# Low halves and the norm's scale and bias in a two-stage trunk: from GpSimd to VectorE

## The chip, the core and the metric

The kernel runs on one NeuronCore of a Trainium2 chip. The metric is the device time of one execution in microseconds (us); the time of a kernel is the median of its timed runs. TensorE (PE) multiplies, VectorE (DVE), ScalarE (ACT) and GpSimd (POOL) work elementwise, SyncE (SP) issues most transfers. Each engine takes its instructions in order; semaphores order the engines among themselves.

## What is computed

A post-norm decoder layer on 512 tokens of 1024 channels: a mixer of three branches, an output projection, a residual and a layer norm; then a two-level mixture of 16 experts, a residual and a second norm. Everything is float32. Cut to what matters here:

```python
def reference(x, mem, ...):
    x = layer_norm(x, ln_in_g, ln_in_b)
    m = hybrid_mixer(x, ...)                      # ends in y @ w_o + b_o
    x = layer_norm(ALPHA * x + m, ln1_g, ln1_b)   # "the norm" of the change
    f = hierarchical_moe(x, w_rg, b_rg, w_re, b_re, w_up, w_down)
    x = layer_norm(ALPHA * x + f, ln2_g, ln2_b)

def hierarchical_moe(x, ...):
    # best of 4 groups, best 2 of its 4 experts, weights from the two softmaxes
    h = silu(x @ w_up[e][:, :256]) * (x @ w_up[e][:, 256:]) * gate[e]
    y = sum over e of h @ w_down[e]
```

## The kernel before

**Split products.** Each float32 matrix is split into a high half (a cast to fp32r, on ScalarE) and a low half (the matrix less its high half). A product is three TensorE passes: high times high, high times low, low times high (`mm3`). For an expert's up weights, four slices of 128x1024, `prep_hi` casts and `prep_lo` subtracts (L691); for its down weights, two slices, `dn_hi` casts and `dn_lo` subtracts (L1142). The tokens of a block are split in `split_xs`, the hidden activations in `h_ev` (both through L82 on ScalarE and L83 on VectorE).

**Output projection and norm.** The loop over `i` from 0 to 7 makes eight tiles of 128 tokens x 512 channels; tile i is half n = i // 4 of token tile i % 4. `wo_mm` issues its 24 multiplications in pieces, `wo_add` (L719) adds the residual on VectorE, `wo_stats` (L725) takes the statistics. One iteration later TensorE transposes the tile (`r_tr`, which therefore waits for `wo_add`) and multiplies it into the router's logits (`router`). From i = 5 on the second half of a token tile t is there, and VectorE makes its inverse deviation (`ln1_stats`), the logits (`logits_a`, `logits_b`), the centering times gain (`center_ops`, L822) and the scale plus bias (`scale_ops`, L826). In the kernel before, only token tile 0 takes that way whole: tile 1 is centered on VectorE, scaled on ScalarE (L873) and biased on GpSimd (L874); tile 2 and three quarters of tile 3 go through `ln1_act`, normed on ScalarE (L837), multiplied by the gain and biased on GpSimd (L838, L839). `put_x1` stores a normed tile twice in device memory: for the gathers, and as the residual of the second norm. `prep_half(0, ...)` prepares expert 0's four slices in iterations 5 and 6, its low halves on GpSimd.

**Routing.** `route_ops` finds the group and the two experts of each token in short chains on VectorE; `rank_mm` counts on TensorE; `pos_ops` makes the positions of the last expert's tokens, the first block's; `pick` multiplies these tokens out of x1 (L812) instead of gathering them. `weave(chain, fill)` issues a chain of small operations with large ones spread between them.

**Experts.** 18 blocks of 128 places follow: experts in `order`, two of them twice. Block b multiplies up (`up_mm`, 24 multiplications L109), transposes the hidden activations of the block before (`h_tr`, L1116), transposes the tokens of the next (`transp`, L1095), and multiplies the block before down (`down_mm`, L1153). In between VectorE and ScalarE prepare the next expert's slices, gate the hidden activations (L1110), and order the remaining experts and tokens by load (`order_experts`, `order_tokens`; L1045 to L1070, L1216 to L1237). GpSimd gathers the tokens of a later block by indices (L1018) and scatters a finished block into the sum in device memory (L1166). In the kernel before it also makes the low halves of slices 0 and 3 of expert 1, of slices 2 and 3 of expert 2, and of the down weights of experts 0 and 1.

**Order.** From L697 on the order is written out by hand (`manual_schedule`): each engine runs what the program lists, in that order. Loads of weights are 1 MB units on SyncE's queue (`load_unit`, L674); a load that reuses a buffer waits for its last reader.

Of the kernel before, what the change touches and what calls it, by code (L numbers as in the profile page):

```python
# [17 lines left out]
P = 128  # L18
D = 1024
# [34 lines left out]
def trunk(ctx, tc, x, mem, rows, cols, wz, wkv, pac, pb8, pb2, wax, ws, wo, wr, br, we, out):  # L54
# [88 lines left out]
    def weave(chain, fill=()):  # L143
        done = 0
        for i, f in enumerate(chain):
            f()
            while done * len(chain) < (i + 1) * len(fill):
                fill[done]()
                done += 1
# [543 lines left out]
    def prep_half(key, i, lo_eng=None):  # L693
        prep_hi(key, i)
        prep_lo(key, i, lo_eng)
# [25 lines left out]
    def wo_stats(i):  # L721
        n, t = divmod(i, NT)
        if n == 0:
            stats[t] = small.tile([P, 2, 6], F32, name="bnst1", bufs=4)
        dve.bn_stats(stats[t][:, n, :], x1[:, t, n * 512:(n + 1) * 512])  # L725
# [95 lines left out]
    def center_ops(t, n, cs):  # L821
        return [lambda c=c: dve.scalar_tensor_tensor(x1[:, t, c:c + n], x1[:, t, c:c + n], mvs[t][:, 0:1], g1[:, c:c + n],  # L822
                                                     op0=ALU.subtract, op1=ALU.mult) for c in cs]
# [5 lines left out]
    def put_x1(eng, t):  # L829
        for d_ in (x1_d, acc_d[0]):  # L830
            eng.dma_start(d_[t * P:(t + 1) * P, :], x1[:, t, :])

    def ln1_act(t, c0):
        nmr = small.tile([P, 1], F32, name="nmr", bufs=2)
        dve.scalar_tensor_tensor(nmr, mvs[t][:, 0:1], -1.0, rstds[t], op0=ALU.mult, op1=ALU.mult)
        hb = x1[:, t, c0:]
        act.activation(hb, hb, AF.Identity, scale=rstds[t], bias=nmr)  # L837
        pool.tensor_tensor(hb, hb, g1[:, c0:], op=ALU.mult)  # L838
        pool.tensor_tensor(hb, hb, b1[:, c0:], op=ALU.add)  # L839

    rest = []
    pending = {NT: [(2, 1)], NT + 1: [(3, 0), (3, 1)], NT + 2: [(4, 0)]}
    for i in range(2 * NT):
        j = i - 1
        t = j - NT
        ps = mmps()
        if i == 6:
            ohe = so2.tile([P, NT, P], F32, name="xr2")
        wo_mm(i, ps, 0, 2)
        if i:  # L850
            r_tr(j)
        if i in (NT + 1, NT + 2):
            for h in range(2):
                prep_half(0, 2 * (i - NT - 1) + h, pool)
        wo_mm(i, ps, 2, 4)
        if i:
            router(j)
        if t == 0:
            weave(ln1_stats(0))
        elif t == 1:  # L860
            weave(ln1_stats(1), scale_ops(0, 256, range(0, D, 256)))
            put_x1(sp, 0)
        elif t == 2:
            ops, r_ = route_ops(0, 2)
            rest += r_
            weave(ops, ln1_stats(2))
        if t >= 0:
            logits_a(t)
            if t < 2:
                weave(center_ops(t, D, (0,)))  # L870
            logits_b(t)
            if t == 1:
                act.mul(x1[:, t, :], x1[:, t, :], rstds[t])  # L873
                pool.tensor_tensor(x1[:, t, :], x1[:, t, :], b1, op=ALU.add)  # L874
                put_x1(sp, t)
            if t == 2:
                ln1_act(t, 0)
                put_x1(sp, t)
        wo_mm(i, ps, 4, 6)
        if t == 2:  # L880
            rank_mm(0)
            rank_mm(1)
            ops, r_ = route_ops(2, 3)
            rest += r_
            weave(ops, pos_ops(0, 2)[:2])
        wo_mm(i, ps, 6, 8)
        for e, u in pending.get(i, ()):
            load_unit(e, u)
        wo_add(i, ps)
        wo_stats(i)  # L890
        if i + 3 < 2 * NT:
            load_xr(i + 3)
    t = NT - 1
# [7 lines left out]
    pick(1, 4, 8)  # L901
    logits_a(t)
    logits_b(t)
    ln1_act(t, 256)
    ops, rest = route_ops(t, NT)
    weave(ops, center_ops(t, 256, (0,)) + scale_ops(t, 256, (0,)))
    put_x1(sp, t)
    pick(2, 0, 4)
    rank_mm(t)
# [47 lines left out]
    xsm = {}  # L957
    xg_ = yp.tile([P, NT, D], F32, name="y")
    xgs = [mo.tile([P, D], F32, name="xg0")] + [xg_[:, i, :] for i in range(2)]
    prep_lo(1, 0, pool)  # L960

    def scratch(shape):
        t = rt.tile([P, 128], F32, name="scr", bufs=2)
# [68 lines left out]
    def order_experts():  # L1032
# [48 lines left out]
        lambda: dve.tensor_copy(whi, wt),  # L1081
        lambda: dve.tensor_copy(val[:, 1], whi.bitcast(F32)),
        lambda: dve.tensor_tensor(val[:, 2], wt, whi.bitcast(F32), op=ALU.subtract),
    ] + vals_s + oe_a, [lambda i=i, c=c: prep_lo(1, i, None, c, c + 512) for i in (1, 2) for c in (0, 512)])
    prep_lo(1, 3, pool)
    load_unit(4, 1)

    def transp(key):
# [153 lines left out]
    for b in range(nb):  # L1242
        p_ = seq[b]
        nxt = seq[b + 1] if b + 1 < nb else p_
        pu = up_mm(b)
        if b == 0:
            dn_hi(0, 0)
            dn_hi(0, 1)
            transp(1)
            pw = map_mm(ohs_s, NS, 1, 3)  # L1250
            gws = map_gw(pw, NS, "s")
        elif b == 1:
            pth = h_tr(h)
        else:
            hT = h_ev(pth)
        if b == 3:
            blk["ixx"] = map_ix(pix, NCOLX, "x")
            gather(5, *where(5)[::2])
            gather(6, *where(6)[::2])
            weave(vals_x)  # L1260
            pwx = map_mm(ohs_x, NCOLX, 1, 3)
        if b == 4:
            blk["gwx"] = map_gw(pwx, NCOLX, "x")
        ix, gw, c = where(b)
        new = [seq[b - 1]] if b and (b == 1 or seq[b - 2] != seq[b - 1]) else []
        if b == nb - 1:
            break

        def dn_prep():
            for p1 in new:  # L1270
                pl = pools[p_] if nxt != p_ else xp if pools[p_] is hlp else hlp
                for n in range(2):
                    if b > 1:
                        dn_hi(p1, n)
                    dn_lo(p1, n, pool if b < 3 else dve, pl)
                if at[p1] + 3 < E:
                    load_unit(order[at[p1] + 3], 2)

        dn_prep()
        tail = []  # L1280
        if b == 1:
            load_unit(order[5], 0)
        if b and nxt != p_:
            for i in range(3):
                prep_hi(nxt, i)
        if 3 < b < nb - 1:
            yb = down_ev(pdn[b - 2])
        held = b > 1 and seq[b - 2] == seq[b - 1]
        if b and nxt != p_:
            if not held:  # L1290
                prep_hi(nxt, 3)
            if b == 1:
                prep_lo(nxt, 2, pool)
                prep_lo(nxt, 3, pool)
                ops = oe_b + order_tokens()
                weave(ops[:8], [lambda i=i, c=c_: prep_lo(nxt, i, None, c, c + 512) for i in range(2) for c_ in (0, 512)])
                hT = h_ev(pth)
                weave(ops[8:18])
                tail = ops[18:]
            else:  # L1300
                ops = []
                if b == 2:
                    ohs_x, ops, vals_x = map_ops(blk["px"], blk["ohx"], NCOLX, "x")
                weave(ops[:5] or [lambda: None] * 3, [lambda i=i: prep_lo(nxt, i) for i in range(3)])
                tail = ops[5:] if held else ops[5:] + [lambda: prep_lo(nxt, 3)]
        if b and nxt != p_:
            for i in (2 * at[p_] + 9, 2 * at[p_] + 10):
                if i < 2 * E:
                    load_unit(order[i // 2], i % 2)
        h = gate_h(pu, gw, c)  # L1310
        if 0 < b < nb - 1:
            transp(b + 1)
        weave(tail)
        if b + 4 < nb and b not in (1, 2):
            gather(b + 4, *where(b + 4)[::2])
        if b == nb - 2:
            gb2 = mlate.tile([P, 2048], F32, name="raw3")
            g2, b2 = gb2[:, :D], gb2[:, D:]

            def load_gb(eng, i):  # L1320
                r = ROWS.index("ln2_g") + i
                eng.dma_start((g2, b2)[i], rows[r:r + 1, :].to_broadcast([P, D]))

            load_gb(sp, 0)
            load_gb(sp, 1)
        if 3 < b < nb - 1:
            scatter(yb, *where(b - 2)[::2], b - 2)
        if b == nb - 4:
            oht = mox.tile([P, 4, T], F32R, name="rawx", bufs=2)
            row_hot(oht[:, 0], *where(nb - 3)[::2])  # L1330
        if b == nb - 3:
            for i in range(1, 3):
                row_hot(oht[:, i], *where(nb - 3 + i)[::2])
        if b:
            pdn[b - 1] = down_mm(b - 1, hT)
            if b == nb - 2:
                ys.append(down_split(pdn[b - 1]))
            elif b < 3:
                scatter(down_ev(pdn[b - 1]), *where(b - 1)[::2], b - 1)
        if b:  # L1340
            pth = h_tr(h)
        if held:
            prep_half(nxt, 3)
        if b == 2:
            pix = map_mm(ohs_x, NCOLX, 0, 1)
# [191 lines left out]
```

## Time and profile before

| | us |
|---|---|
| median of 3 timed runs (lowest, highest) | 967.24 (965.01, 968.96) |
| span of the profiled execution | 964.1 |
| TensorE busy with multiplications | 886.1 |
| VectorE busy | 617.2 |
| ScalarE busy | 456.8 |
| GpSimd busy | 155.6 |

The profile gives no time of the profiled execution apart from its span; the timed runs stand for it. Shares of busy time are averages over stages with different limits, so the stretch of the change (683 to 781 us) is read by itself. A busy engine may also be waiting inside an instruction: an instruction's length has to be held against others of its shape. The granted clock of TensorE is a share of 2.4 GHz; its two levels are 1.2 and 2.4 GHz. A wait is put down to the releaser that came last.

### The profile page before, as it was taken

The numbers are of one execution on the slowest core, as the hardware profiler recorded it, in microseconds if no ns is written. First come the engines' busy times: TensorE is split into PE (matmuls) and PEld (weight loads), VectorE is DVE, ScalarE is ACT, GpSimd is POOL, SyncE is SP. The second block draws the span as 40 slices with busy tenths as digits, with TensorE's granted clock in tenths as the row PEclk, the third lists the DMA queues.
The fourth block names the chain that finished last, engine by engine and source line by source line (L and its number), as shares of the span: only waits on it lengthen the run. The fifth ranks groups of instructions, "written<-read, shape, count | busy, mean of one in ns | idle before, by whom it ended". The sixth has DMA issues, their size and how long they took to land. (4 is left out here: it accounts for less than half of the span.)

```text
span 964.1 us, 11210 instructions
## 1 busy us (share of the span) xinstructions
PE 886.1 (92%) x4260; PEld 739.1 (77%) x4260; DVE 617.2 (64%) x993; ACT 456.8 (47%) x635; POOL 155.6 (16%) x112
## 2 busy tenths in 40 slices
PE   4798999999999999999999999999965789999990
PEld 3586888889988888888788887888865568888880
DVE  6988546225654533345876586663688887689966
ACT  4323342224544342216768668341225347688852
POOL 4322000000000100000000000000436422323843
PEclk9898999999999999999999999999978789999995
DMA  8406223223232613321222221369444577989573
GB/s 342 163 40 226 79 84 118 88 88 131 96 124 88 219 47 109 110 99 55 99 87 99 99 99 60 126 231 379 154 175 160 178 248 259 295 262 401 163 192 106
DMA packets 29867, 148.88 MB, mean 154 GB/s; under 512 B 5538, under 2 KB 5794, under 8 KB 16497
## 3 DMA queue, kind: packets, MB, share of 16 engines
q1 hardware_dynamic: 21312, 128.81, 36.6%
q0 software_dynamic: 7056, 17.12, 6.6%
q10 hardware_dynamic: 1440, 2.19, 0.7%
q8 instruction: 35, 0.57, 0.2%
q14 instruction: 24, 0.19, 0.1%
HBM read 138.33 MB, written 18.35 MB: 163 GB/s over the span
## 5 line engine op out<-in xcount | busy, mean ns | idle before, releaser
L109 PE MATMUL mm<-hl 128*128 128x512 f32 x1440 | 336.3, 392 | 0.0
L109 PEld LDWEIGHTS mm<-hl 128*128 128x128 f32 x1440 | 271.0, 189 | 56.3 <-DVE bnst L114 0.2
L83 DVE TENSOR_TENSOR hl<-raw,hl 128x1024 fp32r<-128x1024 f32 (+1 forms) x117 | 137.9, 1182 | 135.4 <-ACT hl L82 134.7
L82 ACT CAST hl<-raw 128x1024 fp32r<-128x1024 f32 (+1 forms) x117 | 117.8, 1017 | 132.9 <-PE mm L109 120.8
L109 PE MATMUL mm<-o,hl 128*128 128x512 f32 x624 | 142.9, 389 | 1.1 <-ACT o L82 1.1
L109 PEld LDWEIGHTS mm<-o,hl 128*128 128x128 f32 x624 | 117.1, 188 | 25.8 <-ACT o L82 1.5
L109 PE MATMUL mm<-hl,xs 128*128 128x512 f32 x432 | 111.1, 414 | 10.5 <-DVE xs L83 10.5
L109 PEld LDWEIGHTS mm<-hl,xs 128*128 128x128 f32 x432 | 83.7, 198 | 30.6 <-DVE xs L83 11.4
L691 POOL TENSOR_TENSOR hl<-o,hl 128x1024 fp32r<-128x1024 f32 x6 | 15.3, 2557 | 362.7 <-DVE ge L746 361.7
L691 DVE TENSOR_TENSOR hl<-o,hl 128x1024 fp32r<-128x1024 f32 (+1 forms) x46 | 53.3, 1189 | 2.6 <-ACT hl L685 2.6
L1153 PE MATMUL mm<-hl,hT 128*128 128x512 f32 x196 | 50.6, 404 | 1.1 <-DVE hT L83 1.1
L685 ACT CAST hl<-o 128x1024 fp32r<-128x1024 f32 x48 | 48.1, 1053 | 1.7 <-PE mm L1153 1.7
L1153 PEld LDWEIGHTS mm<-hl,hT 128*128 128x128 f32 x196 | 35.6, 189 | 8.9 <-DVE hT L83 1.6
L525 POOL MEMSET zero<- 128x1024 f32 x1 | 1.0, 957 | 241.1 <-PE mm L109 241.1
L222 ACT ACTIVATE gate<-mm,col 128x512 f32<-128x512 f32 x24 | 16.6, 690 | 39.6 <-PE mm L109 39.5
L1133 ACT CAST hl<-raw 128x1024 fp32r<-128x1024 f32 x32 | 32.0, 1054 | 0.0
L1142 DVE TENSOR_TENSOR hl<-raw,hl 128x1024 fp32r<-128x1024 f32 x24 | 28.4, 1225 | 4.9 <-ACT hl L1133 1.9
L109 PE MATMUL mm<-memT,hl 128*128 128x256 f32 x192 | 27.3, 286 | 0.2 <-ACT memT L82 0.2
L301 PE MATMUL mm<-o,hl 128*128 128x512 f32 x96 | 24.7, 414 | 1.8 <-ACT o L293 1.8
L109 PE MATMUL mm<-hl,yh 128*128 128x512 f32 x96 | 25.7, 414 | 0.0
L109 PEld LDWEIGHTS mm<-memT,hl 128*128 128x128 f32 x192 | 24.9, 191 | 0.9 <-ACT memT L82 0.4
L301 PE MATMUL mm<-hl 128*128 128x512 f32 x96 | 24.7, 410 | 0.0
(334 smaller groups left out, 1241.2 us busy)
## 6 DMA issues: line engine op xcount, KB each, us to landing
raw<-in_wz_dram SPq DMA_DIRECT2D x32, 1024.0 KB, 4.7
o<-in_we_dram SPq DMA_DIRECT2D x24, 1024.0 KB, 7.3
raw<-in_we_dram SPq DMA_DIRECT2D x16, 1024.0 KB, 5.9
raw<-in_pac_dram SPq DMA_DIRECT2D x8, 1024.0 KB, 4.7
raw<-in_wkv_dram SPq DMA_DIRECT2D x8, 1024.0 KB, 4.7
rawx<-in_we_dram SPq DMA_DIRECT2D x8, 1024.0 KB, 7.6
raw<-in_pb_dram SPq DMA_DIRECT2D x4, 1024.0 KB, 4.9
raw<-in_wo_dram SPq DMA_DIRECT2D x4, 1024.0 KB, 4.8
```

What stands on the lines that cost most here:

```text
L82: act.copy(hi, src)
L83: dve.tensor_tensor(lo, src, hi.bitcast(F32), op=ALU.subtract)
L109: pe.matmul(ps, lhsT=a(sa_), rhs=b(sb_), start=first and i == 0, stop=last and i == 2)
L222: act.activation(store[j], ps, AF.Sigmoid, bias=cc(C_M + br_i * 8 + j))
L301: pe.matmul(ps, lhsT=xT(k, slice(t * P, (t + 1) * P))(sx), rhs=wv[2 * n + k // 4, k // 2 % 2][:, sw, k % 2, :], start=i == 0, stop=i == 23)
L525: pool.memset(zero, 0.0)
L685: act.copy(t[:, 0], raws[key, i // 2][:, (i % 2) * 1024:(i % 2 + 1) * 1024])
L691: (eng or dve).tensor_tensor(t[:, 1, c0:c1], src[:, c0:c1], t[:, 0, c0:c1].bitcast(F32), op=ALU.subtract)
L1133: act.copy(dnh[key][:, :, n * 512:(n + 1) * 512], dn_half(key, n))
L1142: eng.tensor_tensor(dnl[key][n], dn_half(key, n), dnh[key][:, :, ns].bitcast(F32), op=ALU.subtract)
L1153: pe.matmul(ps, lhsT=hT[:, sa_, f, :], rhs=dn[sb_][:, f, :], start=i + f == 0, stop=i + f == 3)
```

## The change

Elementwise work between the output projection and the third expert block is issued on VectorE, which before was on GpSimd. In the loop of the projection, expert 0's high halves stay where they were and its low halves move to VectorE, behind the addition and statistics of the same iteration. `ln1_act` goes: token tiles 1 to 3 are all centered with `center_ops` and scaled with `scale_ops` in halves of 512 columns (tile 3's centering too), so ScalarE's passes over them go as well. In the expert stage `prep_lo(1, 0)` and `prep_lo(1, 3)`, `prep_lo(2, 2)` and `prep_lo(2, 3)`, and `dn_lo` of experts 0 and 1 go to VectorE, with slice 2 of expert 2 woven into the ordering chain and slice 3 behind it. GpSimd keeps the gathers and scatters.

```diff
--- before.py
+++ after.py
@@ -830,14 +830,6 @@
         for d_ in (x1_d, acc_d[0]):
             eng.dma_start(d_[t * P:(t + 1) * P, :], x1[:, t, :])
 
-    def ln1_act(t, c0):
-        nmr = small.tile([P, 1], F32, name="nmr", bufs=2)
-        dve.scalar_tensor_tensor(nmr, mvs[t][:, 0:1], -1.0, rstds[t], op0=ALU.mult, op1=ALU.mult)
-        hb = x1[:, t, c0:]
-        act.activation(hb, hb, AF.Identity, scale=rstds[t], bias=nmr)
-        pool.tensor_tensor(hb, hb, g1[:, c0:], op=ALU.mult)
-        pool.tensor_tensor(hb, hb, b1[:, c0:], op=ALU.add)
-
     rest = []
     pending = {NT: [(2, 1)], NT + 1: [(3, 0), (3, 1)], NT + 2: [(4, 0)]}
     for i in range(2 * NT):
@@ -851,7 +843,7 @@
             r_tr(j)
         if i in (NT + 1, NT + 2):
             for h in range(2):
-                prep_half(0, 2 * (i - NT - 1) + h, pool)
+                prep_hi(0, 2 * (i - NT - 1) + h)
         wo_mm(i, ps, 2, 4)
         if i:
             router(j)
@@ -866,15 +858,10 @@
             weave(ops, ln1_stats(2))
         if t >= 0:
             logits_a(t)
-            if t < 2:
-                weave(center_ops(t, D, (0,)))
+            weave(center_ops(t, D, (0,)))
             logits_b(t)
-            if t == 1:
-                act.mul(x1[:, t, :], x1[:, t, :], rstds[t])
-                pool.tensor_tensor(x1[:, t, :], x1[:, t, :], b1, op=ALU.add)
-                put_x1(sp, t)
-            if t == 2:
-                ln1_act(t, 0)
+            if t:
+                weave(scale_ops(t, 512, (0, 512)))
                 put_x1(sp, t)
         wo_mm(i, ps, 4, 6)
         if t == 2:
@@ -888,6 +875,9 @@
             load_unit(e, u)
         wo_add(i, ps)
         wo_stats(i)
+        if i in (NT + 1, NT + 2):
+            for h in range(2):
+                prep_lo(0, 2 * (i - NT - 1) + h)
         if i + 3 < 2 * NT:
             load_xr(i + 3)
     t = NT - 1
@@ -901,9 +891,8 @@
     pick(1, 4, 8)
     logits_a(t)
     logits_b(t)
-    ln1_act(t, 256)
     ops, rest = route_ops(t, NT)
-    weave(ops, center_ops(t, 256, (0,)) + scale_ops(t, 256, (0,)))
+    weave(ops, center_ops(t, 512, (0, 512)) + scale_ops(t, 512, (0, 512)))
     put_x1(sp, t)
     pick(2, 0, 4)
     rank_mm(t)
@@ -957,7 +946,6 @@
     xsm = {}
     xg_ = yp.tile([P, NT, D], F32, name="y")
     xgs = [mo.tile([P, D], F32, name="xg0")] + [xg_[:, i, :] for i in range(2)]
-    prep_lo(1, 0, pool)
 
     def scratch(shape):
         t = rt.tile([P, 128], F32, name="scr", bufs=2)
@@ -1081,8 +1069,9 @@
         lambda: dve.tensor_copy(whi, wt),
         lambda: dve.tensor_copy(val[:, 1], whi.bitcast(F32)),
         lambda: dve.tensor_tensor(val[:, 2], wt, whi.bitcast(F32), op=ALU.subtract),
-    ] + vals_s + oe_a, [lambda i=i, c=c: prep_lo(1, i, None, c, c + 512) for i in (1, 2) for c in (0, 512)])
-    prep_lo(1, 3, pool)
+    ] + vals_s + oe_a, [lambda i=i, c=c: prep_lo(1, i, None, c, c + 512) for i in (0, 1) for c in (0, 512)])
+    prep_lo(1, 2)
+    prep_lo(1, 3)
     load_unit(4, 1)
 
     def transp(key):
@@ -1272,7 +1261,7 @@
                 for n in range(2):
                     if b > 1:
                         dn_hi(p1, n)
-                    dn_lo(p1, n, pool if b < 3 else dve, pl)
+                    dn_lo(p1, n, dve, pl)
                 if at[p1] + 3 < E:
                     load_unit(order[at[p1] + 3], 2)
 
@@ -1290,13 +1279,11 @@
             if not held:
                 prep_hi(nxt, 3)
             if b == 1:
-                prep_lo(nxt, 2, pool)
-                prep_lo(nxt, 3, pool)
                 ops = oe_b + order_tokens()
                 weave(ops[:8], [lambda i=i, c=c_: prep_lo(nxt, i, None, c, c + 512) for i in range(2) for c_ in (0, 512)])
                 hT = h_ev(pth)
-                weave(ops[8:18])
-                tail = ops[18:]
+                weave(ops[8:18], [lambda c=c_: prep_lo(nxt, 2, None, c, c + 512) for c_ in (0, 512)])
+                tail = ops[18:] + [lambda: prep_lo(nxt, 3)]
             else:
                 ops = []
                 if b == 2:
```

## Rows read from the trace of the kernel before

**Rows 1.** The page's first line: span of the profiled execution.

```profile
span 964.1 us, 11210 instructions
```

**Rows 2.** Windows: length, busy PE, PEld, DVE, ACT, POOL, PEclk, DMA share, GB/s.

```profile
683.20:733.80 50.60, 37.72 (x208) 33.24 (x206) 44.49 (x136) 13.85 (x18) 23.66 (x10) 0.83 0.46 172
733.80:781.20 47.40, 31.75 (x143) 24.86 (x144) 42.88 (x86) 23.77 (x35) 24.59 (x13) 0.84 0.57 195
781.20:940.00 158.80, 158.80 (x750) 129.88 (x751) 127.42 (x158) 115.17 (x171) 61.94 (x47) 0.98 0.82 263
```

**Rows 3.** TensorE's waits, 680 to 785: line, releaser, total, times, longest us.

```profile
PE mm L109 <- DVE xs L83: 10.5, 1, 10.5
PE aux L732 <- DVE y L719: 6.9, 2, 3.5
PE aux L802 <- DVE cnt L788: 5.2, 1, 5.2
```

**Rows 4.** Timeline, block 0 to 1 (start, us, engine, line, tiles, [idle before <-releaser]).

```profile
739.35 3.20 DVE L691 TENSOR_TENSOR hl<-o,hl 128x512 fp32r<-128x512 f32 x1
...
741.06 1.06 PE L1095 MATMUL aux<-ident,xg 128*128 128x128 f32 x8 [1.18 <-DMA xg<-x_d,ixg]
...
742.78 10.07 DVE L1053 TENSOR_TENSOR scr<-scr,iof 128x121 f32<-128x121 f32 x1
...
743.46 4.65 POOL L1142 TENSOR_TENSOR yb<-raw,hl 128x1024 fp32r<-128x1024 f32 x2
...
748.08 4.63 POOL L691 TENSOR_TENSOR hl<-rawx,hl 128x1024 fp32r<-128x1024 f32 x2
...
754.01 7.91 PE L109 MATMUL mm<-hl,xs 128*128 128x512 f32 x22 [10.53 <-DVE xs L83]
```

**Rows 5.** VectorE by line and shape (busy us, mean ns), 785:900, then 655:735.

```profile
L691 DVE TENSOR_TENSOR hl<-o,hl 128x1024 fp32r<-128x1024 f32 x28 | 33.1, 1219 | 2.6 <-ACT hl L685 2.6
...
L822 DVE SCALAR_TENSOR_TENSOR y<-y,bnmv,g 128x1024 f32<-128x1024 f32 x2 | 2.6, 1278 | 0.0
...
L774 DVE TENSOR_TENSOR scr<-ge 128x16 f32<-128x16 f32 x2 | 0.3, 175 | 0.0
```

**Rows 6.** Timeline, last two projection tiles.

```profile
693.54 4.74 POOL L691 TENSOR_TENSOR hl<-o,hl 128x1024 fp32r<-128x1024 f32 x2 [0.98 <-ACT hl L685]
693.66 2.29 DVE L135 SCALAR_TENSOR_TENSOR lnr<-lnt,lnr 128x1 f32<-128x1 f32 x1
...
695.88 2.69 DVE L826 SCALAR_TENSOR_TENSOR y<-y,lnr,b 128x256 f32<-128x256 f32 x1
...
702.55 1.83 DVE L774 TENSOR_TENSOR scr<-ge 128x32 f32<-128x32 f32 x1
...
708.84 2.33 DVE L774 TENSOR_TENSOR scr<-ig 128x16 f32<-128x16 f32 x1
...
711.62 1.99 DVE L787 TENSOR_SCALAR r<-rk 128x4 f32<-128x4 f32 x1
```

**Rows 7.** Timeline, routing of the last token tile.

```profile
721.41 1.87 DVE L826 SCALAR_TENSOR_TENSOR y<-y,lnr,b 128x256 f32<-128x256 f32 x1
...
723.21 1.77 DVE L774 TENSOR_TENSOR scr<-ig 128x16 f32<-128x16 f32 x1
...
725.01 2.26 DVE L776 TENSOR_TENSOR scr<-scr,thr 128x16 f32<-128x16 f32 x1
```

**Rows 8.** Timeline, block 2.

```profile
767.87 5.31 DVE L1234 TENSOR_TENSOR t<-t,fl 128x8 f32<-128x8 f32 x1
```

**Rows 9.** The line L826 by itself: duration ns min/median/max.

```profile
L826 DVE SCALAR_TENSOR_TENSOR y<-y,lnr,b x5: 479/934/2690, 691.9 to 721.4; 128x256 f32<-128x256 f32 x5
```

**Rows 10.** TensorE's timeline: picks at two clocks, block 0's up multiplications.

```profile
708.98 2.05 PE L812 MATMUL mm<-xr,y 128*128 128x128 f32 x16
...
727.97 4.97 PE L812 MATMUL mm<-xr,y 128*128 128x128 f32 x24
...
733.77 6.11 PE L109 MATMUL mm<-hl,xs 128*128 128x512 f32 x24
```

## The prediction

> **What bounds the kernel now.** I read the page's span first: the profiled execution spans 964.1 us [rows 1]; the median of the timed runs is 967.2, so some 3 us lie around the span, and I take them as unchanged. Then I cut the stretch around the change into three windows [rows 2]. From 781.2 to 940 TensorE is busy in all of its 158.8 us: that part of the expert stage is bound by TensorE, and nothing in it changes code, so whatever arrives earlier at 781 should arrive earlier at the end. From 683 to 781 it is different: TensorE is busy 37.7 of 50.6 us and 31.8 of 47.4 us, so it stands idle for 28.5 us, and its granted clock is 0.83 and 0.84 there. VectorE is busy 44.5 and 42.9 us of these. GpSimd does 23.7 and 24.6 us; all of the first and two thirds of the second (the rest are gathers and scatters) is the work that the change takes away from it.
>
> TensorE's waits say who is late [rows 3]: every large one ends on VectorE. They are 10.5 us for the low half of the second block's tokens, 6.9 us in two waits for the additions behind the output projection, 5.2 us for the routing counts of the last token tile.
>
> The last view is the timeline. In it VectorE's busy time is mostly waiting. L1053 is a multiplication of 128x121 elements and takes 10.07 us [rows 4]; an operation of 128x16 takes 0.175 us and one of 128x1024 takes 1.22 us [rows 5]. It ends at 752.85, and the four GpSimd subtractions beside it end at 752.71 [rows 4]. The same holds at every stretched operation: in the last two projection tiles L135 on one column takes 2.29 us and L826 takes 2.69 us beside two GpSimd subtractions that end at 698.28, L774 takes 1.83 and 2.33 us, L787 takes 1.99 us [rows 6]; in the last token tile L826 takes 1.87, L774 1.77, L776 2.26 us [rows 7]; L1234, on 128x8, takes 5.31 us [rows 8]. I read this as one mechanism: a VectorE instruction of this kind that falls beside a GpSimd elementwise instruction waits until that one has ended.
>
> **The change part by part.** Prices on VectorE: a low half of a weight slice (128x1024) is 1.22 us, a subtract-and-multiply of 1024 columns 1.28 us [rows 5], one of 256 columns 0.48 us (the shortest of L826) [rows 9]. One of 512 columns, which the trace does not show, lies between 0.48 and half of 1.28 plus a fixed part, so between 0.5 and 0.8; I take 0.65, since two of them make the same columns as the 1.28. What a stretched operation gives back is its length less 0.2 us (0.5 for L826).
>
> Step A, up to the addition of the seventh projection tile (L719). Goes: 2.1 (L135) + 2.2 (L826) = 4.3 us [rows 6]. Comes: two low halves of expert 0, now behind the statistics of tile 5, 2.4 us, and the scale of token tile 1 in two halves, 1.3 us. Net gain 0.6 us.
>
> Step B, up to the addition of the last projection tile. Goes: 1.6 + 2.1 + 1.8 = 5.5 us [rows 6]. Comes: the other two low halves 2.4, centering and scaling token tile 2, 1.3 + 1.3 us; 0.15 goes with the small product for ScalarE. Net 0.6 us. Both steps are on the path: TensorE waited 6.9 us for just these additions [rows 3]. Since large operations overlap their neighbours by about 0.1 us, I take A and B together as 1.5 us, with -0.5 and 3 as ends.
>
> Step C, the routing chain of the last token tile, for which TensorE waits 5.2 us [rows 3]. Goes: 1.4 + 1.6 + 2.1 = 5.1 us [rows 7]. Comes: four operations of 512 columns (2.6 us) for two of 256 (1.0 us). Net 3.5 us.
>
> TensorE's clock. After these waits it ran slow: 24 multiplications that pick tokens take 4.97 us, 16 of the same shape took 2.05 us earlier, which is 3.1 us for 24 [rows 10]; so 1.9 us lie in that group alone, and as much again in the picks and the router ahead of it. With waits of 2 us instead of 3.5 and 5.2 some of this comes back. Between 0 and 3.7 us I take 1.5.
>
> Step D, block 0 to block 1 of the experts. Goes: 2.5 us of the 3.20 us low half at 739.35, and 9.9 of L1053 [rows 4]. Comes: two whole low halves of expert 1 that GpSimd did, 2.4 us. Net 10.0 us, all on TensorE's 10.5 us wait. The tokens of block 1 reach TensorE at 741.1 [rows 4] and VectorE would come to them at 743.4 (the low half of 739.35 ends at 740.0, four small operations take about 1.0, two low halves 2.4), so the gather is not the next bound, by 2.3 us.
>
> Step E, block 1 to block 2. VectorE gets two low halves of the down weights (2.4 us) and one of the up weights in two pieces (1.3 us). These lie beside block 1's 24 up multiplications. Those (22 of them behind the wait) took 7.91 us at the low clock [rows 4], against 6.11 for all 24 in block 0 [rows 10], so 2.3 us go on TensorE. VectorE becomes late by 1 to 2 us here. Net 0.5 us, ends -2 and 1.5. If the cover by the multiplications were gone, the cost would be the whole 3.7 us.
>
> Step F, block 2 to block 3. Goes: 5.1 us of L1234 [rows 8]. Comes: the last low half of expert 2 (1.2) and two low halves of the down weights of expert 1 (2.4). Net 1.5 us.
>
> Costed at nothing: the transfers. The stores of the normed tokens and the loads of weights stand on SyncE's queue in the old order; the two loads that reuse the buffers of expert 0 now wait for VectorE's low halves, about 1 us later than for GpSimd's, and their experts (3 and 4) come over 40 us later. GpSimd keeps its gathers and scatters and has nothing in front of them. ScalarE loses three passes over the tokens.
>
> Sum: 1.5 + 3.5 + 1.5 + 10.0 + 0.5 + 1.5 = 18.5 us. The span becomes 945.6, the time 967.2 - 18.5 = 948.7 us.
>
> **The rivals.** (1) VectorE is the saturated engine and gets slower. It is busy 87.4 of 98 us in the two stretches [rows 2], so 10.6 us are free, and the change brings it 3.7 + 5.0 + 1.6 + 2.4 + 3.7 + 3.6 = 20.0 us. If the stretched operations were not stretched by GpSimd's arithmetic but by something that stays (its gathers, say), 20.0 - 10.6 = 9.4 us would be added: 977. It decides if less than 9.4 of the 32 us of stretch vanish. Against it: L1053 and the 2.69 us of L826 end within 0.3 us of the end of GpSimd's subtractions [rows 4, 6], and from 785 to 900, with gathers and scatters alone on GpSimd, the 28 low halves of one group average 1.219 us [rows 5].
>
> The Trainium skill (Perfetto Trace Analysis, "Optimizing Scalar/DVE Operations") says that with VectorE saturated, giving work to GpSimd may make sense, which speaks against this change; it adds that the two share an SBUF read port, so that it might not help. By its first half the time is rival 1's; the rows side with its second half.
>
> (2) Weights become late. The stretch from 733.8 to 781.2 moves 195 GB/s in 47.4 us; in 35.4 us the same bytes need 261 GB/s, and the next stretch moves 263 with TensorE never waiting [rows 2]. So it should just fit. If it doesn't, VectorE and ScalarE wait for slices and about half the gain goes: 958.
>
> (3) The clock holds. If TensorE runs at 2.4 GHz throughout, the picks and the router give 2.2 us more, and the window from 781, granted 0.98 [rows 2], holds some 6.4 us at half speed (4% of 158.8), which cost 3.2 us; I count 2.3 of them: gain 23, time 944. For it: the waits that come before each slow part shrink. Against it: waits of 1 to 2 us on VectorE stay in every step.
>
> **How the numbers follow.** Forecast 0.60, the held clock 0.23, late weights 0.12, slower 0.05. The range takes in the forecast's ends (A and B down by 2, clock down by 1.5, E down by 2.5 give 12.5 us of gain; the upper ends give about 23), rival 3 and part of rival 2: 941 to 957. A change of 0.5% (4.8 us) is about what a measurement can tell. Faster 0.92, same 0.03 (the worst of the late weights), slower 0.05.
>
> **What would show it.** Right: L1053, L1234, L774, L776 at 0.2 to 0.3 us; TensorE's wait for the second block's low half under 1.5 us; the window from 781 on as long as before, only earlier; VectorE's work up by 20 us but its busy time in the stretch down. Step A and B right: the seventh and last additions come 0.5 to 3 us earlier. Wrong: long VectorE operations beside gathers, TensorE waiting on slices of weights after the third block, or a wait for the hidden activations (L1116 or L1153) of several us in blocks 1 and 2, which would mean that step E or F costs more.

## The result, and the profile after

| | before | after |
|---|---|---|
| median of the timed runs, us | 967.15 (4 runs) | 943.43 (4 runs: 940.93 to 946.66) |
| ratio | | 0.977, 95% interval 0.975 to 0.979 |
| span of the profiled execution, us | 964.1 | 939.1 |

The change makes the kernel 23.7 us faster; the prediction said 18.5 (948.7, range 941 to 957). Five more runs of the changed kernel, taken later, gave 941.6 to 948.9 with a median of 947.8 beside 964.5 for the kernel before: 16.7 us, ratio 0.981 (0.978 to 0.985). The median of all nine is 944.2; the mean granted clock of the five up to 944.2 us is 0.976 to 0.978, that of the four from 946.7 us on 0.971 to 0.974. The two profiled executions of the changed kernel agree better: by the table below and the one of the experiments the stretch behind the fifth addition became 24.0 and 23.1 us shorter.

The place where the change begins is itself loose. The fifth projection addition (L719 of the fifth tile) lies ahead of all that the change touches:

```profile
683.26 0.69 DVE L719 TENSOR_TENSOR y<-mm,xr 128x512 f32<-128x512 f32 x1 [5.39 <-PE mm L109]
```

is the kernel before, and of the kernel after the span and the same instruction are

```profile
span 939.1 us, 11191 instructions
...
682.29 0.69 DVE L719 TENSOR_TENSOR y<-mm,xr 128x512 f32<-128x512 f32 x1 [5.39 <-PE mm L109]
```

so 1.0 us of the 25.0 us between the spans were there already. In the thirteen profiles of this study that instruction lies between 680.8 and 685.8. All of this scatter comes from the first 111 us: from VectorE's fourth instruction of line L410, at 106 to 111 us, to the fifth addition it is 574.7 us in every one of them. From here on all stretches are counted from it.

| us from the fifth addition to | before | after | gained in the step | predicted |
|---|---|---|---|---|
| the seventh addition | 17.7 | 16.3 | 1.4 | A: 0.6 |
| the eighth, last addition | 30.5 | 27.6 | 1.5 | B: 0.6 (A and B: 1.5) |
| block 0's up multiplications | 50.5 | 40.5 | 7.1 | C and the clock: 5.0 |
| block 1's, behind their wait | 70.8 | 50.6 | 10.2 | D: 10.0 |
| block 2's | 82.5 | 61.7 | 0.6 | E: 0.5 |
| block 3's | 98.0 | 75.3 | 1.9 | F: 1.5 |
| block 4's | 110.9 | 87.2 | 1.0 | rival 3 only |
| the end | 280.8 | 256.8 | 0.3 | 0 |

Windows of the kernel after that answer to [rows 2] (window, length, busy time of TensorE, its weight loads, VectorE, ScalarE, GpSimd, granted clock, share of the transfer engines, GB/s):

```profile
682.20:722.50 40.30, 34.21 (x206) 29.29 (x204) 36.50 (x144) 10.34 (x15) 0.00 (x0) 0.92 0.58 215
722.50:757.50 35.00, 29.37 (x145) 22.94 (x144) 34.12 (x96) 23.76 (x35) 8.38 (x6) 1.00 0.75 263
757.50:915.00 157.50, 157.50 (x749) 128.87 (x750) 127.07 (x158) 115.14 (x171) 62.36 (x47) 0.99 0.81 265
```

The last window is full of multiplications as before, 157.5 us against 158.8, only earlier. The two ahead of it are 22.7 us shorter together; the clock in them rose from 0.83 and 0.84 to 0.92 and 1.00. VectorE has 20 us more work there, by the prediction's sum, and is busy for 70.6 instead of 87.4 us.

TensorE's waits, which answer to [rows 3] (who waits, for whom: total, times, longest, us; L1105 is L1116 of before):

```profile
PE aux L802 <- DVE cnt L788: 3.0, 1, 3.0
PE aux L1105 <- DVE h L1099: 2.6, 2, 1.9
PE aux L732 <- DVE y L719: 2.0, 1, 2.0
...
PE mm L109 <- DVE xs L83: 0.5, 1, 0.5
```

The 10.5 us for block 1's low half are 0.5, the 6.9 us for the additions 2.0, the 5.2 us for the counts 3.0.

Lines of VectorE's timeline that answer to [rows 4, 6, 7, 8] (L1041 is L1053 of before, L1223 is L1234):

```profile
697.26 1.41 DVE L826 SCALAR_TENSOR_TENSOR y<-y,lnr,b 128x512 f32<-128x512 f32 x2
...
702.29 0.14 DVE L774 TENSOR_TENSOR scr<-ge 128x32 f32<-128x32 f32 x1
...
708.93 0.17 DVE L774 TENSOR_TENSOR scr<-ig 128x16 f32<-128x16 f32 x1
...
709.55 0.17 DVE L787 TENSOR_SCALAR r<-rk 128x4 f32<-128x4 f32 x1
...
717.28 0.17 DVE L774 TENSOR_TENSOR scr<-ig 128x16 f32<-128x16 f32 x1
...
729.11 0.29 DVE L1041 TENSOR_TENSOR scr<-scr,iof 128x121 f32<-128x121 f32 x1
...
746.09 0.17 DVE L1223 TENSOR_TENSOR t<-t,fl 128x8 f32<-128x8 f32 x1
```

The multiplication of 128x121 takes 0.29 us instead of 10.07, L1223 0.17 instead of 5.31, L774 0.14 and 0.17 instead of 1.83, 2.33 and 1.77. The two scales of 512 columns, whose price the trace of before did not show, take 1.41 us for both.

TensorE's timeline, for the clock [rows 4, 10]:

```profile
718.88 2.92 PE L812 MATMUL mm<-xr,y 128*128 128x128 f32 x24
...
732.84 5.43 PE L109 MATMUL mm<-hl,xs 128*128 128x512 f32 x22 [0.47 <-DVE xs L83]
...
757.54 7.41 PE L109 MATMUL mm<-hl,xs 128*128 128x512 f32 x24
```

The 24 picks take 2.92 us instead of 4.97, block 1's 22 up multiplications 5.43 instead of 7.91, and block 3's, 8.43 in the kernel before, 7.41.

### The profile page after: what moved, and what is told of

Its sections match the earlier page's. It is cut to its first block, busy times and chain, and to the rows that moved or that the text cites. A ratio compares the mean times of both kernels' runs of the same rounds, so it can differ in the third digit from the quotient of the medians.

```text
span 939.1 us, 11191 instructions
## 1 busy us (share of the span) xinstructions
PE 880.2 (94%) x4260; PEld 733.2 (78%) x4260; DVE 600.0 (64%) x1011; ACT 452.8 (48%) x632; POOL 116.0 (12%) x95
## 5 line engine op out<-in xcount | busy, mean ns | idle before, releaser
L109 PE MATMUL mm<-hl 128*128 128x512 f32 x1440 | 336.2, 392 | 0.0
L109 PE MATMUL mm<-hl,xs 128*128 128x512 f32 x432 | 107.5, 404 | 0.5 <-DVE xs L83 0.5
L109 PEld LDWEIGHTS mm<-hl,xs 128*128 128x128 f32 x432 | 81.0, 191 | 19.5 <-DVE xs L83 1.1
L691 DVE TENSOR_TENSOR hl<-o,hl 128x1024 fp32r<-128x1024 f32 (+1 forms) x52 | 57.8, 1143 | 2.6 <-ACT hl L685 2.6
L1142 PE MATMUL mm<-hl,hT 128*128 128x512 f32 x196 | 50.6, 404 | 0.6 <-DVE hT L83 0.6
L1131 DVE TENSOR_TENSOR hl<-raw,hl 128x1024 fp32r<-128x1024 f32 x26 | 30.7, 1223 | 4.3 <-PE mm L109 2.0
L733 ACT COPY x1T<-aux 128x512 f32<-128x512 f32 x8 | 4.7, 587 | 44.0 <-PE aux L732 24.0
```

The costliest lines, as they stand in the source:

```text
L109: pe.matmul(ps, lhsT=a(sa_), rhs=b(sb_), start=first and i == 0, stop=last and i == 2)
L691: (eng or dve).tensor_tensor(t[:, 1, c0:c1], src[:, c0:c1], t[:, 0, c0:c1].bitcast(F32), op=ALU.subtract)
L733: act.copy(x1T.rearrange("p k n -> p (k n)"), ps)
L1131: eng.tensor_tensor(dnl[key][n], dn_half(key, n), dnh[key][:, :, ns].bitcast(F32), op=ALU.subtract)
L1142: pe.matmul(ps, lhsT=hT[:, sa_, f, :], rhs=dn[sb_][:, f, :], start=i + f == 0, stop=i + f == 3)
```

## The experiments

All distances are again from the fifth addition. Each line of the table is one profiled execution; the medians come from the timed runs, with the kernel before at 965.9 (first four), 966.4 (next three) and 964.5 (last four) beside them.

| kernel | last addition | last count issued | block 0 | block 1 | block 3 | block 4 | end | median |
|---|---|---|---|---|---|---|---|---|
| before | 30.5 | 44.5 | 50.5 | 70.8 | 98.0 | 110.9 | 280.8 | 967.2 |
| after | 27.6 | 36.3 | 40.5 | 50.6 | 75.3 | 87.2 | 256.8 | 943.4 |
| norm_only | 27.6 | 38.4 | 44.0 | 56.2 | 87.9 | 100.8 | 270.7 | 955.2 |
| experts_only | 30.8 | 41.1 | 47.2 | 57.4 | 82.1 | 94.0 | 263.9 | 948.8 |
| low0_pool | 30.0 | 38.8 | 44.4 | 54.5 | 79.2 | 91.1 | 260.5 | 947.9 |
| low0_early | 23.7 | 32.5 | 39.4 | 49.2 | 74.0 | 87.0 | 256.5 | 940.9 |
| idle_reads | 27.6 | 36.3 | 40.5 | 50.5 | 81.0 | 91.4 | 260.9 | 947.3 |
| idle_writes | 27.6 | 36.4 | 40.5 | 50.5 | 75.7 | 87.6 | 257.9 | 943.0 |
| filler | 30.6 | 43.0 | 47.1 | 67.7 | 94.8 | 107.6 | 277.1 | 964.0 |
| after_again | 27.6 | 36.3 | 40.5 | 50.5 | 75.2 | 87.1 | 257.7 | 947.8 |
| early_again | 23.7 | 32.5 | 38.1 | 48.0 | 72.9 | 85.7 | 255.5 | 941.2 |
| after_filler | 27.6 | 36.4 | 40.5 | 50.5 | 75.2 | 87.1 | 256.4 | 942.8 |
| early_filler | 23.7 | 32.5 | 36.6 | 46.6 | 71.3 | 81.7 | 251.5 | 936.2 |

From block 4's up multiplications to the end every one of them takes 169.3 to 170.6 us. What is gained by then stays, and nothing is gained behind it.

### Is it GpSimd's reading that stops VectorE?

idle_reads: the changed kernel, with four GpSimd instructions that no instruction waits for.

```diff
     gather(3, ixg, NS - 4)
+    spare = xg_[:, 3, :]
+    pool.memset(spare, 1.0)
...
             gather(b + 4, *where(b + 4)[::2])
+        if b == 0:
+            for _ in range(4):
+                pool.tensor_tensor(spare, spare, spare, op=ALU.mult)
```

> The changed kernel, and in block 0, behind the fourth gather, GpSimd squares a spare tile of 128x1024 four times. Nothing reads the tile and nothing waits for these four instructions, so by the order of the data they cost nothing. Theory (a VectorE instruction with two tensors of the on-chip memory waits until GpSimd's elementwise instructions have ended): VectorE's first low half of the down weights, at about 734, stands still for some 8 us and the hidden activations of block 0 come late: 6 to 9 us slower than the changed kernel, 949 to 952. Rival (the delays before were waits for GpSimd's results): no difference, 943.

Ratio to the kernel before 0.980 (0.976 to 0.984), median 947.3; its end lies 4.1 us later than that of the changed kernel. GpSimd's, VectorE's and TensorE's lines (L1133 is `dn_lo`, L1144 `down_mm`):

```profile
735.77 9.96 POOL L1307 TENSOR_TENSOR y<-y 128x1024 f32<-128x1024 f32 x4
...
736.85 4.75 DVE L1133 TENSOR_TENSOR yb<-raw,hl 128x1024 fp32r<-128x1024 f32 x2
741.52 1.86 DVE L1048 TENSOR_SCALAR nx<-ntot 128x16 f32<-128x16 f32 x1
...
743.90 1.86 DVE L1049 SCALAR_TENSOR_TENSOR tab<-tab,nx 128x16 f32<-128x16 f32 x1
...
748.95 1.22 PE L1144 MATMUL mm<-hl,hT 128*128 128x512 f32 x2 [6.44 <-DVE hT L83]
...
766.06 5.87 PE L109 MATMUL mm<-hl,xs 128*128 128x512 f32 x24
```

Two low halves that take 2.36 us take 4.75, two operations on 128x16 take 1.86 each instead of 0.17: 5.8 us in all, and TensorE waits 6.44 us for block 0's hidden activations, 0.64 in the changed kernel. So GpSimd's arithmetic stretches VectorE's instructions with no data passing between the engines. The size was off: I expected 6 to 9 us. Here the two engines alternated, one GpSimd instruction for one of VectorE's, and block 3's up multiplications ran at the full clock (5.87 us), which gave 1.5 us back.

idle_writes: the same place, ten fills instead.

```diff
+        if b == 0:
+            for _ in range(10):
+                pool.memset(spare, 1.0)
```

> As the run with four squarings, but GpSimd fills the spare tile ten times with a constant instead (0.96 us each in the kernel before, so about the same 9.6 us of busy GpSimd). Theory (it is GpSimd's reading that stops VectorE): no difference, 943, and VectorE's low halves of the down weights at 1.2 us. Rival (any busy GpSimd stops VectorE): as the run with squarings, 949 to 952.

```profile
734.48 10.09 POOL L1307 MEMSET y<- 128x1024 f32 x10
...
735.59 2.35 DVE L1133 TENSOR_TENSOR yb<-raw,hl 128x1024 fp32r<-128x1024 f32 x2
737.86 0.67 DVE L1048 TENSOR_SCALAR nx<-ntot 128x16 f32<-128x16 f32 x1
...
742.75 0.83 DVE L1060 TENSOR_SCALAR eix<-eidf 128x8 int32<-128x8 f32 x1
```

GpSimd is busy for 10.09 us and the low halves beside it take their 2.35 us; the median is 943.0. Two `tensor_scalar` operations notice (0.67 and 0.83 instead of 0.17 us), and two multiplications right behind the second end with it. So for the low halves it is not a busy GpSimd that counts but one that reads. The Trainium skill (SBUF — State Buffer, "Who interferes with whom") says that a VectorE instruction with two inputs in SBUF, the on-chip memory, contends with a GpSimd instruction that reads it, and not with one that only writes; both runs agree, 4.75 against 2.35 us. The stretched instructions are not only of that kind: L787 (1.99 us [rows 6]) and L1048 (1.86 us in idle_reads) are `tensor_scalar` operations with one tensor to read.

### The two halves of the change

norm_only is the changed kernel with the expert stage's five places back at the kernel before:

```diff
+    prep_lo(1, 0, pool)
...
-                    dn_lo(p1, n, dve, pl)
+                    dn_lo(p1, n, pool if b < 3 else dve, pl)
...
+                prep_lo(nxt, 2, pool)
+                prep_lo(nxt, 3, pool)
```

and likewise for expert 1: slice 3 goes back to GpSimd (`prep_lo(1, 3, pool)`), and slice 2 takes the place of slice 0 in VectorE's woven chain.

> Only the part up to the first expert block (expert 0's low halves, the norm's scale and bias) goes to VectorE; the expert stage keeps GpSimd's subtractions. Theory (each GpSimd elementwise instruction stops VectorE for its length, parts add up): the gain of steps A to C with the faster clock, 10.0 us up to block 0's up multiplications, and the 10.07 us multiplication in block 0 stays long: 967.2 - 10 = 957, range 955 to 959. Rival (the later wait swallows an earlier start, for instance because gathers or weights set block 1): under 4 us gained, 963 or more.

Median 955.2, ratio 0.990 (0.987 to 0.993): the size came true, the way did not. Lines of GpSimd, VectorE and TensorE:

```profile
714.11 2.35 POOL L691 TENSOR_TENSOR hl<-o,hl 128x1024 fp32r<-128x1024 f32 x1 [389.17 <-DVE lnt L133]
714.16 2.31 DVE L135 SCALAR_TENSOR_TENSOR lnr<-lnt,lnr 128x1 f32<-128x1 f32 x1
...
739.26 4.75 POOL L1131 TENSOR_TENSOR yb<-raw,hl 128x1024 fp32r<-128x1024 f32 x2
...
743.95 4.74 POOL L691 TENSOR_TENSOR hl<-rawx,hl 128x1024 fp32r<-128x1024 f32 x2
...
740.37 8.36 DVE L1047 TENSOR_SCALAR nx<-ntot 128x16 f32<-128x16 f32 x1
...
721.76 4.55 PE L812 MATMUL mm<-xr,y 128*128 128x128 f32 x24
...
752.61 1.14 PE L1142 MATMUL mm<-hl,hT 128*128 128x512 f32 x2 [4.43 <-DVE hT L83]
```

Only 6.5 us are gained at block 0, for two reasons: GpSimd's first low half of expert 1 at 714.11 falls on the inverse deviation of the last token tile (L135, 2.31 us), so that the last count is issued 2.1 us later than in the changed kernel, and the 24 picks run slowly (4.55 us). And the long multiplication of block 0 is gone, though GpSimd's work there is untouched: the same four subtractions now stretch a later instruction, L1047, 8.36 us on 128x16, which lies behind the split of block 1's tokens instead of ahead of it. Block 1 starts 14.6 us earlier than before, and 4.43 us of that go into the wait for the hidden activations. Which instruction is hit, and so who waits, depends on a few us.

experts_only is the complement, the kernel before with the expert stage's part of the diff.

> Only the expert stage's low halves go to VectorE; the projection and the norm stay as before. Theory: the gain of steps D to F and of block 3's clock, 10.2 + 0.6 + 1.9 + 1.0 = 13.7 us: 953.5, range 951.5 to 956. Rival (block 0's delay comes from the gathers that remain): VectorE's multiplication of 128x121 stays several us long and under 5 us are gained. The two parts together should give the 23.7 us of the whole change within 2 us; if they fall short by more, the parts depend on each other through the clock.

```profile
722.12 5.02 PE L812 MATMUL mm<-xr,y 128*128 128x128 f32 x24
...
738.19 5.42 PE L109 MATMUL mm<-hl,xs 128*128 128x512 f32 x22 [1.46 <-DVE xs L83]
```

Median 948.8, ratio 0.984 (0.981 to 0.987): 17.1 us by the medians and 16.9 in the profile, more than the expected range (951.5 to 956) allows. The picks stay slow (5.02 us). The surplus is 3.3 us at block 0: a part of step C belongs to the expert stage, since the 2.26 us of L776 [rows 7] lay beside its first low half; and the router ran at the full clock. The parts sum to 27.1 us in the profiles and the whole to 24.0. The table shows where the 3.1 us too many come from: at block 0 the parts agree with the whole (6.5 + 3.3 for 10.0 us), but from block 0 to block 3 norm_only takes 43.9 us and the kernel before 47.5, though the change touches nothing there in norm_only. There GpSimd's subtractions fall on other instructions, L1047 instead of L1053, and that is worth these 3.6 us.

### Expert 0's low halves

low0_pool undoes one piece:

```diff
         if i in (NT + 1, NT + 2):
             for h in range(2):
-                prep_hi(0, 2 * (i - NT - 1) + h)
+                prep_half(0, 2 * (i - NT - 1) + h, pool)
...
-        if i in (NT + 1, NT + 2):
-            for h in range(2):
-                prep_lo(0, 2 * (i - NT - 1) + h)
```

> The changed kernel with one part undone: expert 0's four low halves are again GpSimd's, in iterations 5 and 6, everything else as changed. Theory: VectorE loses 4.7 us of work and gets back the stretch beside four GpSimd subtractions: about 1.9 us hidden behind TensorE in iteration 5, 2.1 + 2.2 us in iteration 6 and nothing in iteration 7, so the seventh addition comes 2 us later and the last one is even: 943 to 945, within 1 us of the changed kernel. Rival (GpSimd's subtraction costs VectorE nothing where VectorE has other work, so that moving these four was a loss): 4 us or more faster than the changed kernel, 939 or less.

```profile
695.88 2.33 DVE L135 SCALAR_TENSOR_TENSOR lnr<-lnt,lnr 128x1 f32<-128x1 f32 x1
698.13 2.69 DVE L826 SCALAR_TENSOR_TENSOR y<-y,lnr,b 128x256 f32<-128x256 f32 x1
...
705.29 1.11 PE L732 MATMUL aux<-ident,y 128*128 128x128 f32 x4 [4.82 <-DVE y L719]
...
710.53 0.17 DVE L749 TENSOR_TENSOR ge<-ge,aux 128x20 f32<-128x20 f32 x1 [0.69 <-PE aux L740]
...
713.36 0.16 DVE L806 SCALAR_TENSOR_TENSOR pos<-aux,cnt 128x2 f32<-128x2 f32 x1 [0.97 <-PE aux L802]
...
724.54 4.46 PE L812 MATMUL mm<-xr,y 128*128 128x128 f32 x24
```

The seventh addition comes 2.8 us later, as it should, but the last one is not even: 2.4 us later. From the seventh to the last it takes 10.9 us without VectorE's two low halves and 11.25 with them, so taking them away saves 0.35 us there and not 2.4: TensorE has to transpose the seventh tile and run the router and the counts in that time, and VectorE waits for it, 0.69 and 0.97 us. The picks run slowly again (4.46 us). In the profile the end lies 2.8 to 3.7 us behind those of the changed kernel's two profiles. The median is 947.9, outside the expected 943 to 945, but its ratio, 0.980 (0.976 to 0.983), does not stand clear of the changed kernel's 0.977 and 0.981. So the rival, a loss by moving these four, has fallen, and the trace shows a gain of about 3 us that the medians alone do not.

low0_early moves them to where VectorE waits for TensorE:

```diff
-        if i in (NT + 1, NT + 2):
+        if i in (NT, NT + 1):
             for h in range(2):
-                prep_hi(0, 2 * (i - NT - 1) + h)
+                prep_hi(0, 2 * (i - NT) + h)
...
+        if i in (NT, NT + 1):
+            for h in range(2):
+                prep_lo(0, 2 * (i - NT) + h)
         wo_add(i, ps)
         wo_stats(i)
-        if i in (NT + 1, NT + 2):
-            for h in range(2):
-                prep_lo(0, 2 * (i - NT - 1) + h)
```

> The changed kernel with expert 0's high and low halves one iteration earlier, 4 and 5 instead of 5 and 6, the low halves ahead of the addition of the tile, where VectorE waits for TensorE. Theory (VectorE's order sets the additions of the last two projection tiles): the seventh addition comes 1.6 us earlier, when TensorE is ready, the last one 2 to 3 us earlier; 2 to 3.5 us gained on the changed kernel: 940 to 941.5. Rival (TensorE's picks and router set the pace there, not VectorE): no difference, 943.

> Expert 0's halves one iteration earlier, once more beside the changed kernel. Theory (the last count comes 3.9 us earlier, but a slow clock behind it takes most of that back, as in its first profile: 5.47 instead of 2.92 us for the 24 picks): 0.5 to 2.5 us faster than the changed kernel. Rival (the slow picks were a chance of that one execution): 3 to 4 us faster.

> The changed kernel once more, as the mark for the three runs beside it: 942 to 945. Its fifth projection addition may lie some us from where it lay before (that place differed by 5 us between the profiles so far), with the distance from there to the end within 1.5 us of the 256.8 of its first profile.

Medians 940.9 and 941.2, ratios 0.974 (0.973 to 0.976) and 0.976 (0.974 to 0.978), beside 943.4 and 947.8 for the changed kernel, whose interval in its second set is wide (0.981, 0.978 to 0.985). The first median lies in the expected range, but by luck: the profile shows 0.3 us to the end where 2 to 3.5 were expected. The second pair of medians lies 6.6 us apart, which neither expectation had, and the distances of its profiles 2.2 us. In this kernel low halves lie ahead of the fifth addition too, but it still waits 1.03 us for TensorE and comes 6.81 us behind the fourth, as everywhere, so the distances stay comparable. TensorE in the first profile, and then in the second:

```profile
718.48 0.17 PE L802 MATMUL aux<-cnt,low 128*128 128x16 bf16 x1 [3.03 <-DVE cnt L788]
718.51 5.47 PE L812 MATMUL mm<-xr,y 128*128 128x128 f32 x24
...
697.84 0.66 PE L732 MATMUL aux<-ident,y 128*128 128x128 f32 x4 [0.27 <-DVE y L719]
...
715.26 4.34 PE L812 MATMUL mm<-xr,y 128*128 128x128 f32 x24
...
755.40 8.34 PE L109 MATMUL mm<-hl,xs 128*128 128x512 f32 x24
```

The seventh addition is there when TensorE asks (0.27 us of wait), the last count 3.9 us earlier. Then the picks take 4.34 us (5.47 in the first profile, 2.92 in the changed kernel) and block 3 8.34 instead of 7.40: in the two profiles 1.1 and 2.4 us are left at block 0, and 0.2 and 1.4 at block 4. VectorE set the pace there, and the clock took most of it back. The wait ahead of the picks is 3.0 us in the changed kernel and in both of these, so its length alone does not decide how the picks run.

### The clock

filler: the kernel before, VectorE and GpSimd untouched, with idle multiplications in two of TensorE's waits.

```diff
     pick(0, 0, 8)
+    filler(12)
     r_tr(2 * NT - 1)
...
     pick(2, 0, 4)
+    filler(18)
     rank_mm(t)
```

> The kernel before, with multiplications whose result nobody reads put into two of TensorE's waits: 12 behind the first picks (a wait of 3.4 us) and 18 ahead of the last count (a wait of 5.2 us); VectorE and GpSimd are unchanged. Theory (the slow clock behind these waits comes from the waits): the router behind takes 0.96 instead of 1.73 us, the 24 picks 3 instead of 5 us, 2 to 4 us gained: 963 to 965. Rival (the slow clock has another cause): the same lengths as before and no gain, 967 or a little more.

```profile
718.91 0.97 PE L740 MATMUL aux<-wrg,x1T 128*128 128x20 f32 x8
...
728.46 2.92 PE L812 MATMUL mm<-xr,y 128*128 128x128 f32 x24
...
732.32 6.01 PE L109 MATMUL mm<-hl,xs 128*128 128x512 f32 x24
```

The router takes 0.97 instead of 1.73 us, the picks 2.92 instead of 4.97; block 0 comes 3.4 us earlier, with the last addition where it was. The median is 964.0, ratio 0.998 (0.996 to 1.000): 2.3 us by the medians, 3.7 in the profile. So these two waits, left empty, cost the kernel before about 3.4 us beyond their own length.

after_filler and early_filler put 11 such multiplications ahead of the last count, and 7 ahead of block 2's transposition of its hidden activations, into the changed kernel and into low0_early:

```diff
     pick(2, 0, 4)
+    filler(11)
     rank_mm(t)
...
+        if b == 2:
+            w_ = dnh[seq[1]]
+            filler(7, w_[:, 0, :P], w_[:, 0, :512])
         if b:
             pth = h_tr(h)
```

> The changed kernel with multiplications that nobody reads in two of TensorE's waits: 11 ahead of the last count (a wait of 3.0 us) and 7 ahead of block 2's transposition of its hidden activations (a wait of 1.9 us). Theory (the slow clock behind a wait comes from the wait): the picks stay at 2.9 us, block 3's up multiplications fall from 7.4 to 5.9 us: 1.5 us faster than the changed kernel, if the distance shows at the end. Rival (the clock of block 3 has another cause): no difference, or up to 0.5 us slower where the filling overruns the wait.

> Both: expert 0's halves one iteration earlier, and the two fillings. Theory: the picks at 2.9 us and block 3's up multiplications at 5.9 us, so the 3.9 us that the last count comes earlier stay: 4 to 5.5 us faster than the changed kernel, 938 to 939.5. Rival (the fillings don't lift the clock here): as without them, 0.5 to 2.5 us faster.

after_filler:

```profile
721.47 0.17 PE L802 MATMUL aux<-cnt,low 128*128 128x16 bf16 x1 [0.50 <-DVE cnt L788]
...
757.96 0.44 PE L1112 MATMUL aux<-ident,h 128*128 128x128 f32 x2 [0.24 <-DVE h L1106]
...
760.07 7.39 PE L109 MATMUL mm<-hl,xs 128*128 128x512 f32 x24
```

early_filler:

```profile
713.92 2.92 PE L812 MATMUL mm<-xr,y 128*128 128x128 f32 x24
...
750.39 0.44 PE L1112 MATMUL aux<-ident,h 128*128 128x128 f32 x2 [0.26 <-DVE h L1106]
...
752.50 5.87 PE L109 MATMUL mm<-hl,xs 128*128 128x512 f32 x24
```

In after_filler the waits are filled (0.50 and 0.24 us left) and block 3's up multiplications take 7.39 us as without: the theory that the wait right ahead of them slows them has fallen, and the profile's distance to the end is that of the changed kernel within 1.3 us. Its median, 942.8, lies beside 943.4 and 947.8 for the changed kernel and decides nothing. In early_filler both are fast, 2.92 and 5.87 us, with a granted clock of 1.00 from 684 to 780 us, and the 3.9 us stay: median 936.2, ratio 0.971 (0.969 to 0.974), beside 0.981 (0.978 to 0.985) for the changed kernel on the same chip. This version beats both kernels.

## Why the prediction was right, and where it was off

**What bounds.** Right: VectorE's low halves are stretched by a GpSimd that reads and not by one that fills (idle_reads, idle_writes), the short operations that were stretched take 0.14 to 0.29 us after, and everything ahead of block 4 reached the end.

**Steps C, D, E and F** were sized right. In C, from the last token tile's logits to the count's arrival, 8.4 us became 4.9: 3.5 as predicted. D 10.2 for 10.0, E 0.6 for 0.5, F 1.9 for 1.5. In E the mechanism came as told: block 1's 22 up multiplications became 2.5 us shorter (2.3 taken), and two new waits for VectorE's hidden activations, 0.64 and 0.79 us, took part of it back.

**Steps A and B** measured 2.9 us where 1.5 was taken, just inside its upper end of 3. Both gave 0.8 to 0.9 us more than taken. Putting VectorE's work on the path was right: between these additions it is idle for 0.7 us at most, before and after. The terms were small by some tenths each: in A one more stretched L826, of 0.93 us [rows 9], became 0.47, which the sum leaves out, and the new operations took 3.6 us for the 3.7 counted; in B the three stretched operations gave 5.7 us for the 5.5 counted, and the new ones took 4.8 for 5.0. The rest is idle time and overlaps. That the second pair of low halves costs 0.35 us by low0_pool says something else: without it TensorE would set the pace there.

**The clock** was the term most undersized: 1.5 us taken with 3.7 as the upper end, and what is left of the 7.1 us at block 0 after C is 3.6; another 1.0 us came from block 3's up multiplications, which the sum left out and rival 3 held. That the clock has to do with the waits was right for the router and the picks of the kernel before (filler). But the length of the wait ahead does not settle it: behind 3.0 to 3.1 us the 24 picks take 2.92 us in the changed kernel, 4.46 in low0_pool and 5.47 in low0_early; and for block 3 it is open. The measured 943.4 us lies nearer to rival 3's 944 than to the forecast's 948.7. That it lies so near is partly chance: TensorE's clock did not hold (0.92 in the first window), rival 3's further gain of 2.3 us from block 3 on came to 1.0, and 1.4 us of the outcome are A and B, which that rival left alone. So the outcome is the forecast with most of rival 3 in it: 18.5 + 1.4 + 2.1 (clock up to block 0) + 1.0 + 1.0 (the small remainders of D, E, F and the end) = 24.0 us.

**Rival 1** predicted 977 from VectorE's 20 us of new work. The Trainium skill (Perfetto Trace Analysis, "Optimizing Scalar/DVE Operations") has both the advice for it, that giving work to GpSimd may make sense when VectorE is saturated, and the reservation that the SBUF read port that the two share may spoil it; the case is one for the reservation: VectorE's busy time in the two windows fell by 16.8 us with that work added. And beside the gathers and scatters, which stay, no VectorE instruction between 680 and 800 us of the changed kernel's trace is long for its shape.

**Rival 2**, late weights: TensorE is busy in all of the 157.5 us from 757.5 to 915, and the stretch from block 0 to block 3 moves 263 GB/s, as the prediction's sum had it would have to (261).

**The transfers and the gathers**, costed at nothing, stayed so: TensorE waits 1.3 us for block 1's first tokens, 1.2 before.

**What stays open.** Why block 3's up multiplications run slowly in after_filler (granted clock 0.77 in them) and fast in early_filler and idle_reads (1.00). And what makes the first 111 us differ by 5 us; in the two profiles of the changed kernel that is 2.5 of the 3.4 us between their spans. How much of the spread of the other timed runs it makes is not shown, since they left no trace.

## What to carry to other kernels

Where an engine is busy, hold each instruction's length against others of its shape before taking the busy time as work: some 32 us of VectorE's 87 were waits beside GpSimd, and moving 20 us of work onto the busy engine made it less busy. An elementwise operation on GpSimd that takes 2.35 us and stops VectorE meanwhile is worth less than the 1.2 us that VectorE needs for it, so give GpSimd such work only where VectorE has none of the operations that were stretched here: those that read two tensors, and `tensor_scalar`. And cost a shortened wait on TensorE together with the clock behind it: in the kernel before, filling two waits brought block 0 forward by 3.4 us, and with expert 0's halves earlier a slow clock took up to 2.8 of 3.9 us.

## What the runs showed of the hardware that I had not expected

One VectorE instruction can stand behind several GpSimd instructions in a row: L1053 stood through all four (10.07 us), and L1047 in norm_only for 8.36 us; in idle_reads four GpSimd instructions were each let past one by one (4.75, 1.86 and 1.86 us). No run shows what decides between the two. GpSimd filling a tile for 10.09 us did not slow VectorE's subtractions at all (2.35 us for two), but it did slow `tensor_scalar` operations (0.67 and 0.83 instead of 0.17 us). And TensorE's picks ran at either clock behind a wait of the same 3.0 us.
